# Output products of a recurrence in two runs, short operands padded to the whole array, and modulation products of two loads together

## The chip, the cores and the metric

The kernel runs on one core of one Trainium2 chip. The metric is the device time of one execution in microseconds (us). A core has a matrix engine (TensorE, "PE" in the profile), a vector engine (VectorE, "DVE"), a scalar engine (ScalarE, "ACT"), a general engine (GpSimd, "POOL") and SyncE ("SP"), which here only issues transfers between main memory and the on-chip buffer. The engines run side by side, each works through its own list of instructions in order, and they wait for each other on semaphores. TensorE multiplies a stationary operand, loaded first (weight load, "PEld"), with a moving one and writes into accumulator banks (PSUM).

## The reference

One layer of a decoder step for 256 prompt tokens and 8 samples of 8 tokens: 320 token columns in all, with D = 2048 channels and 16 heads of 64. In short:

```
mod = silu(c) @ w_ada + b_ada                     # six vectors: shift, scale, gate for mixer and FFN
h   = rms_norm(x) * (1 + scale_m) + shift_m
z   = h @ w_in                                    # columns of all branches, 9472 wide
r, k, v, decay, a, g = ...                        # token-shifted columns, two low-rank factors of width 64
kk  = k * k_k / norm over the head                # removal keys
per token: S = S*diag(w) - (S kk)(a*kk)^T + v k^T ;  o = S r          # state per head, 64 x 64
y_a = (group_norm(o) + bonus) * g @ w_branch_a
y_b = (gelu(u) * (W_s @ layer_norm(gelu(v)) + b)) @ w_branch_b
x   = x + gate_m * ((sig0*y_a + sig1*y_b) @ w_out)
x   = x + gate_f * FFN(rms_norm(x) ...)           # SwiGLU, width 5632
y   = rms_norm(x)
```

It returns the outputs, the states after the step, the token-shift rows and the normalised v rows of the samples.

## The kernel before

Channels lie on the 128 partitions and tokens on the free axis. A float32 product with a weight matrix is made of three passes over exact high and low parts (L155 to L157): `wsplit` (L133) makes the high part of a loaded weight tile on ScalarE (wh) and the low part on VectorE (wl). A weight tile is up to 1 MB, there are three buffers for tiles (wst) and four for each of the parts. These *main products* have 128 x 128 stationary tiles and 320 moving columns.

The program has these stages. First the modulation of the mixer, the transposed input (L378) and the projection to the recurrence's columns. Then quantities per token (`prep1` to `prep3`, L685 to L805): decay and rate from low-rank factors (L691, L692), sums over a head for the norms of the removal keys (L721) and their return to all rows (L735). Then the recurrence, in chunks of 64 tokens: chunk 4 holds all samples, chunks 0 to 3 the prompt. For a chunk, `chunk_load` fetches what `prep3` wrote to main memory; `chunk_g` makes causal products of keys and queries, two heads' halves at a time on either half of the partitions (L896, L897); `chunk_w` turns keys and values to have tokens on partitions (L910, L915, L916); `chunk_t` completes a triangular inverse (L933, L938); `chunk_x` applies the state and the inverse (L950, L956); `chunk_o` makes the outputs, the state's part and the chunk's own part for each of 8 pairs of heads and each half (L977, L978); `chunk_s` advances the state (L966); `chunk_n` is the group norm (L166). Last come branch b, branch a, the output projection and the FFN.

Between these steps `fill(n)` (L1074) puts quarter units of main products into the program, so that TensorE has work while a chain of small steps runs on other engines, and in proportion it takes from the list `adas` the loads of the other four modulation vectors: `ada_group` (L344) and `ada_cols` (L305), 16 loads of 1 MB for each vector; behind each load stand four products, one for each quarter of the array's columns (L318). Some of these loads are taken out one by one around the norm ahead of the FFN (L1313, L1324) and in its first units (L1412).

The order in each engine's list isn't that of the text: a planner sets it when the program is built, by executing it on its own model of costs and taking what is ready by priority. A block under `manual_schedule` keeps the written order among its own instructions on the named engines; where other instructions fall between stays the planner's. Transfers issued by `ld` stand in SyncE's list, those by `sd` in GpSimd's; each list is worked through in order, so an issue that waits for its buffer holds back all behind it. A tile of a pool (`tag`, `bufs`) takes one of `bufs` buffers and waits until an earlier owner is done.

Of the kernel before, what the change touches and what calls it, by code (L numbers as in the profile page):

```python
# [13 lines left out]
F32 = mybir.dt.float32  # L14
# [35 lines left out]
# columns of the two packed parameter tiles  # L50
# [5 lines left out]
def body(ctx, tc, I, O):  # L56
    """Channels lie on partitions and tokens on the free axis: columns 0..255 are the prompt, 256 + 8*s + t the
    samples.  A float32 product with a weight matrix runs as three float32r passes over exact high and low parts."""
# [27 lines left out]
    # ------------------------------------------------------------------ constants  # L86
# [34 lines left out]
    # ------------------------------------------------------------------ DRAM scratch  # L121
# [10 lines left out]
    # ------------------------------------------------------------------ weights: load, split in two exact parts  # L132
# [30 lines left out]
    def both(ps, w, parts):  # L163
        """ps = w^T (hi + lo), w being exact in float32r"""
# [35 lines left out]
    def tile_units(src, ktiles, xh, xl, group, evict, kx0):  # L200
        """the column tiles of one group, each over all k"""
# [14 lines left out]
    # ================================================================== mixer sub-layer  # L216
# [11 lines left out]
    # ---- conditioning and parameters  # L228
# [6 lines left out]
    ld(xt[0:64, 2], I["x_sample"].rearrange("s t d -> (s t) d"))  # L235
    pr1 = st.tile([128, 128], F32, name="pr1")
# [15 lines left out]
    def params2():  # L252
# [5 lines left out]
        # token-shift states ahead of every sample, zeros ahead of the prompt  # L258
# [8 lines left out]
    # ---- ada: the conditioning rows stationary, four column tiles of the array at once  # L267
# [4 lines left out]
    def ada_half(k0, nk):  # L272
        """shift_m and scale_m of the channel tiles k0..k0+nk-1, nk <= 2: each array tile takes a quarter of k"""
# [31 lines left out]
    def ada_cols(pool, kb, c0s, w, dsts):  # L305
        """array tile j takes w of the modulation columns"""
        box = {}

        def load(kq):
            if kq == 0:  # L310
                box["pa"] = ps_ax(512)
            wt = (pool or late["w"])().tile([128, kb, 4 * w], F32, tag="wa", name="wa", bufs=2)
# [3 lines left out]
            for kk in range(kb):  # L316
                for j in range(4):
                    PE.matmul(box["pa"][32 * j:32 * j + 32, 0:w], cT[:, kq * kb + kk], wt[:, kk, j * w:j * w + w], start=kq + kk == 0, stop=kq * kb + kk == KT - 1,  # L318
                              tile_position=(0, 32 * j))
# [24 lines left out]
    def ada_group(g):  # L344
        """one of the other modulation vectors"""
# [22 lines left out]
    def h_raw(k0, nk):  # L368
        """normalised, channels on partitions"""
# [4 lines left out]
        def turned(k):  # L374
            px = [ps_ax(NP), ps_ax(T - NP)] if k == 0 else [ps_ax(T)] * 2
            for c, n in enumerate(rows):
                o = px[c // 2][:, c % 2 * 128:c % 2 * 128 + n] if k == 0 else px[0][:, c * 128:c * 128 + n]
                PE.transpose(o, xt[0:n, c, k * 128:k * 128 + 128], ident[0:n, 0:n])  # L378
# [22 lines left out]
    # ---- RWKV columns: the sum over k runs in segments, as the modulation arrives  # L401
# [28 lines left out]
    # the groups of four columns in turn, each time over the channel tiles that have come since its last turn  # L430
# [54 lines left out]
    # ------------------------------------------------------------------ main products beside the recurrence  # L485
    mp_g, mpool = open_pool("mp", "left")

    # gMLP constants
    def ws_prep():
# [10 lines left out]
        for s in range(NS):  # L500
            V.tensor_scalar(gp["wsS"][:, :, s], pr[0:64], bm8[0:64, s:s + 1], None, op0=MUL)
# [3 lines left out]
    # bm8[p, s] = 1 where (p mod 64) // 8 == s ; rep8[a, (s, t)] = 1 where a == t  # L505
# [6 lines left out]
    def v_evict(i, ps):  # L512
# [4 lines left out]
        for c, n in enumerate(rows):  # L517
            PE.transpose(pt[0:n, c], gv[:, c * 128:c * 128 + n], ident)
        act(gp["vtm"][:, 0:2, i * 128:i * 128 + 128], pt[:, 0:2], AF.Copy)
        act(gp["vtm"][0:64, 2, i * 128:i * 128 + 128], pt[0:64, 2], AF.Copy)  # L520
# [30 lines left out]
    def gm_open():  # L551
# [3 lines left out]
        gp["wsS"] = gm.tile([64, 8, NS, TS], F32, name="wsS")  # L555
# [907 lines left out]
```

## Time and profile before

| | |
|---|---|
| median of 3 runs | 2081.64 us (2080.64 to 2081.8) |
| profiled execution, first to last instruction (span) | 2079.3 us; its time with start and end isn't listed apart |
| TensorE busy | 2031.0 us, 98%, 14578 products |
| VectorE, ScalarE, GpSimd busy | 51%, 38%, 7% |
| mean granted TensorE clock | 0.984 |
| transfers | 421 MB, 202 GB/s in the mean |

Busy is the time in which at least one instruction of an engine is under way; products overlap, so the distance between starts tells more than a length. "128*64 128x64" is 128 rows and 64 columns of the array, and a moving operand of 128 partitions with 64 columns. An fp32 product stands as two records. Lines named L155 are lines of the kernel; a helper's line (L79, L82) stands for all that it records. In tables of stretches the columns are: stretch, its length, busy time (instructions), granted clock, share of time that the transfer engines were busy, GB/s.

### The profile page before, as it was taken

The numbers are of one execution on the slowest core, as the hardware profiler recorded it, in microseconds if no ns is written. First come the engines' busy times: TensorE is split into PE (matmuls) and PEld (weight loads), VectorE is DVE, ScalarE is ACT, GpSimd is POOL, SyncE is SP. The second block draws the span as 40 slices with busy tenths as digits, with TensorE's granted clock in tenths as the row PEclk, the third lists the DMA queues.
The fourth block names the chain that finished last, engine by engine and source line by source line (L and its number), as shares of the span: only waits on it lengthen the run. The fifth ranks groups of instructions, "written<-read, shape, count | busy, mean of one in ns | idle before, by whom it ended". The sixth has DMA issues, their size and how long they took to land.

```text
span 2079.3 us, 35907 instructions
## 1 busy us (share of the span) xinstructions
PE 2031.0 (98%) x14578; PEld 1860.3 (89%) x14578; DVE 1058.4 (51%) x1904; ACT 794.2 (38%) x1168; POOL 136.6 (7%) x243
## 2 busy tenths in 40 slices
PE   6999999999999999999999999999999999999997
PEld 4788988889787888888888889999999999999997
DVE  2565668759453453445347334445345345445345
ACT  6323376534233233434326233233333332332344
POOL 1000002230330001100000000000000000000000
PEclk9999999999998999999999999999999999999998
DMA  9888447597587757888875775454544454453552
GB/s 273 288 290 299 144 149 256 196 230 214 163 242 196 214 203 242 326 315 292 309 260 180 245 234 173 123 169 128 157 153 145 152 172 126 149 173 123 156 168 71
DMA packets 303109, 420.99 MB, mean 202 GB/s; under 512 B 62310, under 2 KB 202584, under 8 KB 294112
## 3 DMA queue, kind: packets, MB, share of 16 engines
q1 hardware_dynamic: 293856, 388.20, 57.7%
q0 software_dynamic: 9088, 30.50, 4.5%
q8 instruction: 115, 1.88, 0.4%
q14 instruction: 50, 0.41, 0.1%
HBM read 390.40 MB, written 28.23 MB: 201 GB/s over the span
## 4 chain that ended last, share of the span: by engine, by line
PE 86%; issue 4%; DVE 3%; DMA 3%; POOL 1%; SPq 1%; ACT 1%; DVEq 0%; POOLq 0%; ACTq 0%
PE mm L155 25%; PE mm L157 24%; PE mm L156 24%; PE ax L318 4%; PE ax L977 1%; PE ax L978 1%; PE ax L286 1%; DVE wl L79 1%; DMA d_mb<-gt 1%; DMA gt<-d_sg 1%; DMA xt<-in_x_prompt 0%; DVE tm L79 0%; DMA Lr<-d_l 0%; POOL we L1049 0%; PE ax L378 0%
## 5 line engine op out<-in xcount | busy, mean ns | idle before, releaser
L79 DVE TENSOR_TENSOR wl<-ws,wh 128x1024 fp32r<-128x1024 f32 (+1 forms) x304 | 362.7, 1214 | 320.3 <-ACT wh L82 317.6
L82 ACT ACTIVATE wh<-ws 128x1024 fp32r<-128x1024 f32 (+1 forms) x304 | 306.2, 1041 | 462.5 <-PE mm L156 338.3
L155 PE MATMUL mm<-h2h,wh 128*128 128x320 f32 x1408 | 435.9, 310 | 0.7 <-ACT h2h L82 0.7
L156 PE MATMUL mm<-h2l,wh 128*128 128x320 f32 x1408 | 435.1, 309 | 0.1
L157 PE MATMUL mm<-h2h,wl 128*128 128x320 f32 x1408 | 435.1, 309 | 0.0
L79 DVE TENSOR_TENSOR wl<-wf,wh 128x1024 fp32r<-128x1024 f32 x176 | 215.1, 1224 | 327.7 <-ACT wh L82 323.1
L155 PE MATMUL mm<-hh,wh 128*128 128x320 f32 x1184 | 377.0, 320 | 1.2 <-ACT wh L82 0.6
L157 PE MATMUL mm<-hh,wl 128*128 128x320 f32 x1184 | 368.4, 313 | 1.5 <-DVE wl L79 1.4
L156 PE MATMUL mm<-hl,wh 128*128 128x320 f32 x1184 | 369.4, 312 | 0.0
L82 ACT ACTIVATE wh<-wf 128x1024 fp32r<-128x1024 f32 x176 | 185.2, 1058 | 381.9 <-PE mm L156 352.9
L155 PEld LDWEIGHTS mm<-h2h,wh 128*128 128x128 f32 x1408 | 264.1, 188 | 11.7 <-issue 7.5
L156 PEld LDWEIGHTS mm<-h2l,wh 128*128 128x128 f32 x1408 | 264.3, 188 | 0.4 <-DVE h2l L79 0.4
L157 PEld LDWEIGHTS mm<-h2h,wl 128*128 128x128 f32 x1408 | 264.3, 188 | 0.0
L155 PEld LDWEIGHTS mm<-hh,wh 128*128 128x128 f32 x1184 | 224.0, 190 | 31.4 <-issue 22.6
L157 PEld LDWEIGHTS mm<-hh,wl 128*128 128x128 f32 x1184 | 223.9, 190 | 9.8 <-issue 6.3
L156 PEld LDWEIGHTS mm<-hl,wh 128*128 128x128 f32 x1184 | 224.8, 190 | 5.3 <-issue 4.4
L155 PE MATMUL mm<-fh,wh 128*128 128x320 f32 x704 | 217.0, 308 | 0.0
L157 PE MATMUL mm<-fh,wl 128*128 128x320 f32 x704 | 216.8, 308 | 0.0
L156 PE MATMUL mm<-fl,wh 128*128 128x320 f32 x704 | 216.8, 308 | 0.0
L155 PEld LDWEIGHTS mm<-fh,wh 128*128 128x128 f32 x704 | 131.9, 187 | 0.0
L156 PEld LDWEIGHTS mm<-fl,wh 128*128 128x128 f32 x704 | 131.9, 187 | 0.0
L157 PEld LDWEIGHTS mm<-fh,wl 128*128 128x128 f32 x704 | 131.9, 187 | 0.0
(357 smaller groups left out, 2342.7 us busy)
## 6 DMA issues: line engine op xcount, KB each, us to landing
wf<-in_w_ffn_in SPq DMA_DIRECT2D x352, 256.0 KB, 3.0
ws<-in_w_in SPq DMA_DIRECT2D x64, 1024.0 KB, 7.2
wa<-in_w_ada SPq DMA_DIRECT2D x64, 1024.0 KB, 6.3
ws<-in_w_ffn_out SPq DMA_DIRECT2D x40, 1024.0 KB, 5.1
wa<-in_w_ada SPq DMA_DIRECT2D x48, 512.0 KB, 4.9
ws<-in_w_out SPq DMA_DIRECT2D x16, 1024.0 KB, 5.4
d_w<-pk POOLq DMA_DIRECT2D x8, 1120.0 KB, 5.4
wa<-in_w_ada SPq DMA_DIRECT2D x32, 256.0 KB, 4.7
```

The lines of the kernel that those rows point to most:

```text
L79: return (eng or V).tensor_tensor(out, a, b, op=op)
L82: return A.activation(out, in_, fn, **kw)
L155: PE.matmul(ps, hi[:, k, sl], xh[:, kx + a + k], start=f, stop=False)
L156: PE.matmul(ps, hi[:, k, sl], xl[:, kx + a + k], start=False, stop=False)
L157: PE.matmul(ps, lo[:, k, sl], xh[:, kx + a + k], start=False, stop=e)
L286: PE.matmul(box["pa"][32 * j:32 * j + 32, 0:w], cT[:, 4 * q + j], wt[:, j], start=q == 0, stop=q == 3, tile_position=(0, 32 * j))
L318: PE.matmul(box["pa"][32 * j:32 * j + 32, 0:w], cT[:, kq * kb + kk], wt[:, kk, j * w:j * w + w], start=kq + kk == 0, stop=kq * kb + kk == ...
L977: PE.matmul(po[lo:lo + 64, j], SV[:, j, h], b["M"][:, j, h, 64:128], start=True, stop=False)
L978: PE.matmul(po[lo:lo + 64, j], b["VS"][lo:lo + 64, j, h], b["D"][lo:lo + 64, j], start=False, stop=True)
```

## The change

It consists of several edits.

1. In `chunk_o` the output products stand in two runs (all of the state's part, then all of the chunk's own part) into one accumulator bank, in the written order.
2. In `chunk_g` the causal products keep the written order, which alternates the two halves.
3. Operands with fewer than 128 rows or columns are padded with zeros, or with other columns whose results aren't read: the low parts of the low-rank factors, the selection matrices for the head sums and their return, the third token tile of the transposed input and of the transposes in the v branch and at the end, and the gMLP's product for the samples.
4. In `chunk_w` the values of two head pairs are turned by one 128 x 128 transpose; for this `chunk_load` brings them in four transfers in place of one, into one buffer.
5. In `ada_cols` the products of the late modulation wait for two loads and then run together; the loads have three buffers in place of two.
6. Some tiles share buffers (tp, sl, xg, so2), and comments and descriptions go.

The core of the diff (removed comments and the renamed slices that follow from it are left out):

```diff
     def chunk_o(c, SV):
         po = ps_ax(NJ, 64)
-        for j in range(NJ):
-            for h, lo in ((0, 0), (1, 64)):
-                PE.matmul(po[lo:lo + 64, j], SV[:, j, h], b["M"][:, j, h, 64:128], start=True, stop=False)
-                PE.matmul(po[lo:lo + 64, j], b["VS"][lo:lo + 64, j, h], b["D"][lo:lo + 64, j], start=False, stop=True)
+        with tc.manual_schedule(engines={mybir.EngineType.PE}):
+            for j in range(NJ):
+                for h, lo in ((0, 0), (1, 64)):
+                    PE.matmul(po[lo:lo + 64, j], SV[:, j, h], b["M"][:, j, h, 64:128], start=j == 0, stop=False, skip_group_check=True)
+            for j in range(NJ):
+                for h, lo in ((0, 0), (1, 64)):
+                    PE.matmul(po[lo:lo + 64, j], b["VS"][lo:lo + 64, j, h], b["D"][lo:lo + 64, j], start=False, stop=j == NJ - 1, skip_group_check=True)
...
     def chunk_g(c):
-            for jj in range(4):
-                j = 4 * q + jj
+            with tc.manual_schedule(engines={mybir.EngineType.PE}):
+                for jj in range(4):
+                    j = 4 * q + jj
...
     def chunk_load(c):
-        b["v"] = cp.tile([128, NJ, 64], F32, name="vc", tag="vc", bufs=nb)
-        ld(b["v"], d_w[:, c, :, 4])
+        b["v"] = cp.tile([128, NJ // 2, 2, 64], F32, name="vc", tag="vc", bufs=1)
+        for a in range(2):
+            for h in range(2):
+                ld(b["v"][64 * a:64 * a + 64, :, 1 - h], d_w[64 * h:64 * h + 64, c, a::2, 4])
...
     def chunk_w(c):
-        for j in range(NJ):
-            PE.matmul(pv[64:128, j], b["v"][0:64, j], ident[0:64, 0:64], start=True, stop=True)
-            PE.matmul(pv[0:64, j], b["v"][64:128, j], ident[64:128, 64:128], start=True, stop=True)
+        for i in range(NJ // 2):
+            PE.transpose(pv[:, 2 * i:2 * i + 2].rearrange("p j v -> p (j v)"), b["v"][:, i].rearrange("p h t -> p (h t)"), ident)
...
-    def ada_cols(pool, kb, c0s, w, dsts):
-        box = {}
+    def ada_cols(pool, kb, c0s, w, dsts, kr=1, bufs=2):
+        box, held = {}, []
         def load(kq):
-            if kq == 0:
-                box["pa"] = ps_ax(512)
             (the tile, now with bufs=bufs, and its load)
-            for kk in range(kb):
-                for j in range(4):
-                    PE.matmul(box["pa"][32 * j:32 * j + 32, 0:w], cT[:, kq * kb + kk], wt[:, kk, j * w:j * w + w], ...)
+            held.append((kq, wt))
+            if len(held) < kr:
+                return
+            if "pa" not in box:
+                box["pa"] = ps_ax(512)
+            for q, wt in reversed(held):
+                for kk in range(kb):
+                    for j in range(4):
+                        k = q * kb + kk
+                        PE.matmul(box["pa"][32 * j:32 * j + 32, 0:w], cT[:, k], wt[:, kk, j * w:j * w + w], ...)
+            held.clear()
...
     def ada_group(g):
-        return ada_cols(None, 1, [g * D], 512, dsts)
+        return ada_cols(None, 1, [g * D], 512, dsts, kr=2, bufs=3)
...
     def prep1(j):
             PE.matmul(p, ups["h"][:, i, js], lact[i], start=True, stop=False)
-            PE.matmul(p, ups["l"][lo, js], lact[i][lo], start=False, stop=True)
+            PE.matmul(p, ups["l"][:, i, js], lact[i], start=False, stop=True)
...
-        PE.matmul(kn["p"][0:32], hsel[:, j], sq, start=j % 4 == 0, stop=j % 4 == 3)
+        PE.matmul(kn["p"], hsel[:, 2 * NJ - 2 - 2 * j:2 * NJ - 2 - 2 * j + 128], sq, start=j % 4 == 0, stop=j % 4 == 3)
...
-        rs = rp.tile([64, F], F32R, name="rs", tag="rn", bufs=2)
+        rs = rp.tile([128, F], F32R, name="rs", tag="rn", bufs=2)
+        G.memset(rs[64:128].bitcast(F32), 0.0)
...
-            for c, n in enumerate(rows):
-                PE.transpose(o, xt[0:n, c, k * 128:k * 128 + 128], ident[0:n, 0:n])
+            for c in range(3):
+                PE.transpose(o, xt[:, c, k * 128:k * 128 + 128], ident)
...
-        PE.matmul(pm[:, NP:T], gp["vtm"][0:64, 2, sl], gp["wsS"][:, g].rearrange("p s t -> p (s t)"), start=True, stop=True)
+        PE.matmul(pm[:, NP:T], gp["vtm"][:, 2, sl], gp["wsS"][:, g].rearrange("p s t -> p (s t)"), start=True, stop=True)
...
     def turn():                     # v_evict in the same way
-            for c, n in enumerate(rows):
-                PE.transpose(pt[0:n, c], xg[:, c * 128:c * 128 + n], ident)
+            for c, t0 in enumerate((0, 128, T - 128)):
+                PE.transpose(pt[:, c], xg[:, t0:t0 + 128], ident)
-            V.tensor_copy(yy["b"][:, i * 128:i * 128 + 128], pt[0:64, 2])
+            V.tensor_copy(yy["b"][:, i * 128:i * 128 + 128], pt[64:128, 2])
...
-        tp = p2.tile([128, NS, TS], F32, name="tp", tag="tp", bufs=2)
+        tp = p2.tile([128, NS, TS], F32, name="tp", tag="tp", bufs=1)
-                            sl = p2.tile([128, T], F32, name="sl", tag="sl", bufs=2)
+                            sl = p2.tile([128, T], F32, name="sl", tag="hf2", bufs=2)
-                xg = p2.tile([128, T], F32, name="xg", tag="xg", bufs=2)
+                xg = p2.tile([128, T], F32, name="xg", tag="hf2", bufs=2)
-        so = cp.tile([128, NJ, 64], F32, name="so2", tag="so2", bufs=2)
+        so = cp.tile([128, NJ, 64], F32, name="so2", tag="Lc", bufs=1)
```

Memsets on GpSimd write the zeros of the padded parts (of the input tile, of the low factors, of the selection matrices, of the gMLP's v tile and of its sample matrix).

More of the change, by code (lines that the diff above doesn't have):

```diff
@@ L303, in ada_half @@
         return [lambda q=q: load(q) for q in range(4)] + [flush]
-    def ada_cols(pool, kb, c0s, w, dsts):
-        box = {}
+    def ada_cols(pool, kb, c0s, w, dsts, kr=1, bufs=2):
+        box, held = {}, []
         def load(kq):
-            if kq == 0:
-                box["pa"] = ps_ax(512)
-            wt = (pool or late["w"])().tile([128, kb, 4 * w], F32, tag="wa", name="wa", bufs=2)
+            wt = (pool or late["w"])().tile([128, kb, 4 * w], F32, tag="wa", name="wa", bufs=bufs)
             cw = 4 * w // len(c0s)
@@ L315, in load @@
                 ld(wt[:, :, ci * cw:ci * cw + cw], w_ada[kq * kb * 128:(kq + 1) * kb * 128, c0:c0 + cw].rearrange("(k p) n -> p k n", p=128))
-            for kk in range(kb):
-                for j in range(4):
-                    PE.matmul(box["pa"][32 * j:32 * j + 32, 0:w], cT[:, kq * kb + kk], wt[:, kk, j * w:j * w + w], start=kq + kk == 0, stop=kq * kb + kk == KT - 1,
-                              tile_position=(0, 32 * j))
+            held.append((kq, wt))
[7 more added lines that the diff above has]
+                        k = q * kb + kk
+                        PE.matmul(box["pa"][32 * j:32 * j + 32, 0:w], cT[:, k], wt[:, kk, j * w:j * w + w], start=kq == kr - 1 and q == kq and kk == 0,
+                                  stop=kq * kb + kb == KT and q == held[0][0] and kk == kb - 1, tile_position=(0, 32 * j))
+            held.clear()
         def flush():
@@ L516, in v_evict @@
         pt = ps_ax(3, 128)
[L517 to L518 removed]
+        for c, t0 in enumerate((0, 128, T - 128)):
+            PE.transpose(pt[:, c], gv[:, t0:t0 + 128], ident)
         act(gp["vtm"][:, 0:2, i * 128:i * 128 + 128], pt[:, 0:2], AF.Copy)
[L520 removed]
+        act(gp["vtm"][0:64, 2, i * 128:i * 128 + 128], pt[64:128, 2], AF.Copy)
     def v_norm():
@@ L554, in gm_open @@
         gp["wsT"] = gm.tile([128, 8, 128], F32, name="wsT")
-        gp["wsS"] = gm.tile([64, 8, NS, TS], F32, name="wsS")
+        gp["wsS"] = gm.tile([128, 8, NS, TS], F32, name="wsS")
         gp["vtm"] = gm.tile([128, 3, 1024], F32, name="vtm")
+        G.memset(gp["wsS"][64:128], 0.0)
+        G.memset(gp["vtm"][64:128, 2], 0.0)
         gp["wsr"] = gm.tile([128, 8, 128], F32, name="wsr", tag="gA")
@@ L625, in ups_load @@
         ups["h"] = rp.tile([128, 2, 512], F32R, name="uph", tag="uph")
-        ups["l"] = rp.tile([128, 512], F32R, name="upl", tag="upl")
+        ups["l"] = rp.tile([128, 2, 512], F32R, name="upl", tag="upl")
         act(ups["h"], w, AF.Copy)
         for i, lo in enumerate((0, 64)):
-            tt(ups["l"][lo:lo + 64], w[lo:lo + 64, i], ups["h"][lo:lo + 64, i].bitcast(F32), SUB)
+            G.memset(ups["l"][64 - lo:128 - lo, i].bitcast(F32), 0.0)
+            tt(ups["l"][lo:lo + 64, i], w[lo:lo + 64, i], ups["h"][lo:lo + 64, i].bitcast(F32), SUB)
     mG = mpool.tile([128, 2, 2, 64], F32, name="mG")
@@ L698, in prep1 @@
         sg4[j] = lg
-    hsel = rp.tile([128, NJ, 32], F32, name="hsel")
+    hsel = rp.tile([128, 2 * NJ - 2 + 128], F32, name="hsel")
+    G.memset(hsel, 0.0)
     for h, lo in ((0, 0), (1, 64)):
-        G.affine_select(out=hsel[lo:lo + 64], in_=ones[lo:lo + 64, 0:32].unsqueeze(1).to_broadcast([64, NJ, 32]), compare_op=ALU.is_equal, fill=0.0, base=-h, pattern=[[-2, NJ], [1, 32]],
-                        channel_multiplier=0)
+        G.memset(hsel[lo:lo + 64, 2 * NJ - 2 + h:2 * NJ - 1 + h], 1.0)
     bself = rp.tile([64, NJ, 2, 64], F32, name="bself", tag="pk", bufs=2)
-    bsel = rp.tile([64, NJ, 2, 64], F32R, name="bsel")
+    bsel = rp.tile([128, NJ, 2, 64], F32R, name="bsel")
+    G.memset(bsel[64:128].bitcast(F32), 0.0)
     for lo in (0, 32):
@@ L710, in body @@
                             channel_multiplier=1)
[L711 removed]
+    G.tensor_copy(bsel[0:64], bself)
     kn = {}
@@ L1391, in turn @@
             pt = ps_ax(3, 128)
-            for c, n in enumerate(rows):
-                PE.transpose(pt[0:n, c], xg[:, c * 128:c * 128 + n], ident)
+            for c, t0 in enumerate((0, 128, T - 128)):
+                PE.transpose(pt[:, c], xg[:, t0:t0 + 128], ident)
             act(yy["a"][:, :, i * 128:i * 128 + 128], pt[:, 0:2], AF.Copy)
-            V.tensor_copy(yy["b"][:, i * 128:i * 128 + 128], pt[0:64, 2])
+            V.tensor_copy(yy["b"][:, i * 128:i * 128 + 128], pt[64:128, 2])
     pend = []
```

16 lines of the change are left out of this document (7 added, 9 removed).

## The prediction

> **What bounds the kernel now.** I read the page's first parts, then the chain of waits, then TensorE's timeline around the edited lines, and last the transfers.
>
> ```profile
> span 2079.3 us, 35907 instructions
> PE 2031.0 (98%) x14578; PEld 1860.3 (89%) x14578; DVE 1058.4 (51%) x1904; ACT 794.2 (38%) x1168; POOL 136.6 (7%) x243
> PEclk9999999999998999999999999999999999999998
> PE 86%; issue 4%; DVE 3%; DMA 3%; POOL 1%; SPq 1%; ACT 1%; DVEq 0%; POOLq 0%; ACTq 0%
> ```
>
> TensorE is busy for 98% of the span and makes 86% of the chain that ends last; VectorE and ScalarE are far from it. A busy figure says nothing of how well the time is used, so I go by the distance between starts. A microsecond taken out of TensorE's list is worth a microsecond wherever TensorE doesn't then wait for something else.
>
> The five calls of the output product (L977, L978) take these stretches, from the first product to the start of the next other one. The columns are length, TensorE busy with its products, granted clock, transfers' share and rate.
>
> ```profile
> 543.55:553.08 9.53, 9.53 (x65) 0.81 0.41 154
> 648.07:661.64 13.57, 13.57 (x110) 0.64 0.21 74
> 700.88:710.56 9.68, 9.68 (x65) 0.79 0.24 96
> 748.13:757.51 9.38, 9.38 (x65) 0.83 0.01 3
> 784.80:795.66 10.86, 10.86 (x65) 0.67 0.60 231
> ```
>
> That is 53.0 us for 5 x 64 small products (an fp32 product shows as two records; the second stretch also holds some 40 others). Transfers nearly stop in three of them, since the weight buffers are full: TensorE alone is late. The timeline shows why:
>
> ```profile
> 700.88 0.33 PE L977 MATMUL ax<-M,SVp 128*64 128x64 f32 x2
> 701.13 0.33 PE L978 MATMUL ax<-Dt,VS 64*64 64x64 f32 x2
> ```
>
> Each pair takes 0.25 us, and the shape changes from 128x64 to 64x64 each time. Products of the same shapes that stand in a run of 32 are quoted next: 1.15 us to the last one's end.
>
> ```profile
> 722.20 1.15 PE L950 MATMUL ax<-SVp,M 128*64 128x64 f32 x32
> 774.86 1.15 PE L956 MATMUL ax<-xx,Tc 64*64 64x64 f32 x32
> ```
>
> **The change part by part.**
>
> *Output product in two runs.* 32 records of L950's shape, then 32 of L956's: 2 x 1.15 = 2.3 us a chunk, 11.5 for five. The others in the second stretch stay; at full clock I put them at 1.6. So 53.0 - 13.1 = 39.9 us gained. The far end: records that do not overlap at all cost about 0.13 us each (1.05 for eight, quoted below at L896), 8.4 a chunk, a gain of 9. I take the near end, since shape, alternation of the two halves and the one accumulator bank are those of L950 and L956.
>
> *The clock.* Each of the five stretches begins at full clock and loses it after some 4 to 6 us (the 0.64 to 0.83 above). What follows each until the clock is back, added up, and two stretches just before one drop:
>
> ```profile
> sum 16.45, PE 16.45; mean PE 3.29
> 645.10:648.07 2.97, 2.97 (x75) 1.00 0.15 56
> 648.07:651.90 3.83, 3.83 (x36) 1.00 0.02 4
> ```
>
> In these 16.45 us the clock stood at 0.50, so up to 8.2 is lost there; I take 7. The 75 small products in 2.97 us did not cost the clock; the drop came at the end of the second stretch, with 36 in 3.83, at 651.9. The run after the change is of the dense kind and lasts 2.3 us, so I expect no drop. Ends: 0 and 8.2.
>
> *Late modulation, two loads together.* One visit, and the one place where two visits already stand together:
>
> ```profile
> 718.55 0.31 PE L157 MATMUL mm<-hh,wl 128*128 128x320 f32 x1
> 718.79 1.06 PE L318 MATMUL ax<-wa,cT 128*32 128x512 f32 x8
> 719.78 0.42 PE L155 MATMUL mm<-hh,wh 128*128 128x320 f32 x1
> 720.04 0.31 PE L156 MATMUL mm<-hl,wh 128*128 128x320 f32 x1
> ```
>
> ```profile
> 1239.78 1.92 PE L318 MATMUL ax<-wa,cT 128*32 128x512 f32 x16
> 1241.63 0.42 PE L155 MATMUL mm<-h2h,wh 128*128 128x320 f32 x1
> ```
>
> A main product is followed by the next after 0.15 us, but after 0.24 where the shape changes, and the first one behind a visit holds 0.26. So a visit costs 0.09 + 0.99 + 0.11 = 1.19 us, two 2.38; the double one 0.09 + 1.85 + 0.10 = 2.04. 0.34 a pair; four groups of 16 loads are 32 pairs, one already double: 31 x 0.34 = 10.5. The far end, where other work splits the pairs, is 0.
>
> *Operands padded to 128.* The decay and rate products (L691, L692), eight times:
>
> ```profile
> 277.90 0.31 PE L691 MATMUL ax<-lact,uph 128*128 128x328 f32 x1
> 278.14 0.41 PE L692 MATMUL ax<-lact,upl 64*128 64x328 f32 x1
> 278.48 0.42 PE L691 MATMUL ax<-lact,uph 128*128 128x328 f32 x1
> 278.83 0.41 PE L692 MATMUL ax<-lact,upl 64*128 64x328 f32 x1
> 279.18 0.41 PE L155 MATMUL mm<-hh,wh 128*128 128x320 f32 x1
> ```
>
> 1.28 us for four products that in one shape need about 4 x 0.15, and 0.10 on the first main product: 0.78 x 8 = 6.3. The removal key's return product (L735), eight times, is one such 64-row visit: 0.09 + 0.34 + 0.10 against 0.15, so 3.0. Its sums (L721), eight: two changes of shape, about 0.2 each time; 2 with some lost on slower full-width records. The input transposes (16 tiles) and the sample product of the gMLP (8) give up one visit each, 24 x 0.2 = 5. The transposes in the last norm and the v branch already write a full-height tile for two of three thirds; I put them at 0. Together 16.3; the far end is half, if padding slows the records as it may for L721.
>
> *Value transposes.* 80 + 80 products of 64 rows become 20 whole transposes.
>
> ```profile
> L915 PE MATMUL ax<-ident,vc 64*64 64x64 f32 x80 | 5.7, 221 | 0.0
> 624.50 0.61 PE L910 MATMUL ax<-ident,KB 128*128 128x128 f32 x4
> ```
>
> L915 and L916 run beside each other: 5.7 us for both, plus 0.2 a chunk for the changes of shape: 6.7. Four whole transposes 0.54 to 0.61: 5 x 0.54 = 2.7. Gain 4. The Trainium skill speaks against such padding: TensorEngine Tiling (Array Packing), section Key Properties, says that tiles work independently and in parallel, which a whole-array product gives up. The trace bears the rule out inside a run (the 0.11 us for two records below), and by it alone nothing would be gained and the sum would be 4 smaller; here four instructions replace 32, and that decides.
>
> *Causal products in emission order (L896, L897).*
>
> ```profile
> 731.24 0.27 PE L897 MATMUL ax<-M,KB 64*128 64x128 f32 x1
> 731.35 0.27 PE L896 MATMUL ax<-M,KB 64*128 64x128 f32 x1
> ...
> 732.02 1.05 PE L896 MATMUL ax<-M,KB 64*128 64x128 f32 x8
> 733.49 1.13 PE L897 MATMUL ax<-M,KB 64*128 64x128 f32 x8
> ```
>
> Alternating, two records start every 0.11 us; alone, 16 took 2.1. Paired these 16 take 0.9: 1.2 a chunk, 6 for five. Order also binds the first half's products to the later loads of the second; the planner can put main products between, as now. Far end 0.
>
> *What is added.* Three more value loads a chunk, with what queues behind them on SyncE:
>
> ```profile
> 606.52 0.93 SPq L870 DMA_DIRECT2D vc<-d_w  x1
> 600.00:950.00 350.00, 342.28 (x2882) 0.94 0.78 255
> 850.00:900.00 50.00, 49.44 (x337) 1.00 0.89 319
> 0.00:220.00 220.00, 201.66 (x1487) 1.00 0.83 279
> ```
>
> At 0.6 to 0.9 us an issue that is about 2 us of SyncE's queue a chunk, behind which wait the triangular block, the modulation and the weights. It is free where that queue waits anyway; I book 1. The single value buffer is freed by the transposes long before its next load, and the memsets on GpSimd (7% busy) stand early: 0. The shared buffers (tp, sl, xg, so2) change owners between phases: 0. With the modulation in pairs, only a load and no product stands ahead of the FFN norm's sums: one visit less of cover, 1 us. Last, the transfers: 600 to 950 us moves 255 GB/s at a share of 0.78, 273 us of transfers. The terms above shorten that stretch by about 51 (output product 31.5, clock 6, causal 4.8, values 3.2, modulation 5.4), to 299, a share of 0.91. The busiest row ran at 0.89 with TensorE waiting a little; 273 / 0.89 = 307, so I book 8. Ends: 0, and all 51.
>
> **Sum.** 39.9 + 7 + 10.5 + 16.3 + 4 + 6 = 83.7, less 10: 73.7. Span 2079.3 - 73.7 = 2005.6. The execution profiled lies 2.3 us under the runs' median of 2081.64, which I add back: 2008.
>
> **The rivals.**
>
> *Transfers take over (24%).* At the 279 GB/s of the first 220 us, the 89.3 MB of 600 to 950 need 320 us: 21 lost instead of 8, 2021; the limit, no gain there at all, is 2051. For it: the shares above. Against: 319 GB/s with TensorE at 49.44 of 50, and the idle transfers inside the five stretches.
>
> *The clock drops all the same (9%).* Without the 7, and with the five runs at half clock (11.5 more): 2027. The Trainium skill, TensorE: Matmul & The Clock Gate, Part 4, says that transposes do not count as busy, and more of the work is transposes now. The 75 records quoted at clock 1.00 speak against it.
>
> *The planner breaks the runs (6%).* By hand only the order is fixed, not what falls between. With half of the output gain, the causal gain and the pairs gone (20 + 6 + 10.5): 2045. In the second stretch other products already stand inside.
>
> *Slower: pairs hold SyncE's queue (4%).* A modulation load waits for its buffer, and weights wait behind it:
>
> ```profile
> SPq L315 <- PE ax L318: 88.7, 11, 23.9
> wa<-in_w_ada SPq DMA_DIRECT2D x64, 1024.0 KB, 6.3
> ```
>
> That queue already stood 88.7 us in 11 such waits between 600 and 800. If every pair made TensorE wait half a landing (3.2 us), 32 of them cost 101: 2109. It decides from 73.7 / 32 = 2.3 us a pair. Against it: with three buffers a load waits for a pair at least two turns back, no closer than now, and today's waits hardly reach TensorE (2% idle).
>
> **How the numbers follow.** The forecast has 57%, its own range 1998 to 2018. Outside 1996 to 2036 I leave the planner, the slow rival and part of the transfers' tail. Faster holds all but the last rival and a scrap: 0.95; within 0.2% 0.01 (about what a measurement of this kernel can tell from no change); slower 0.04.
>
> **What would show it.** Right: each output product about 2.3 us with one change of shape inside; clock 1.00 from 600 to 800; 32 visits of 16 modulation records at 1.85; no 64-row records on L692's and L735's successors. Wrong: output runs well over 3 us, TensorE waits on weights (wh, wl) in 600 to 950 adding up to over 10 us, or a granted clock of 0.5 right behind the runs.

## The result, and the profile after

| | us, median | lowest to highest | ratio to before, 95% interval |
|---|---|---|---|
| before | 2081.72 | 2080.64 to 2085.22 | |
| after | 2025.81 | 2025.0 to 2027.71 | 0.9727, 0.9713 to 0.974 |
| forecast | 2008 | 1996 to 2036 | 0.965 |

The change is worth 55.9 us, 18 less than forecast. First the head of the changed kernel's profile page.

```profile
span 2023.4 us, 35669 instructions
PE 1964.0 (97%) x14438; PEld 1830.8 (90%) x14438; DVE 1060.0 (52%) x1904; ACT 794.7 (39%) x1168; POOL 141.3 (7%) x254
PEclk9999999999998999999999999999999999999998
```

TensorE is busy for 67.0 us less (2031.0 before), but the span is only 55.9 shorter: outside its busy time there are now 59.4 us, where there were 48.3. That is the first sign of work saved and not cashed.

The output product stands as forecast. Chunk 1 in the timeline (start, length, line, operands, count):

```profile
673.89 1.15 PE L993 MATMUL ax<-M,SVp 128*64 128x64 f32 x32
674.97 1.15 PE L996 MATMUL ax<-Dt,VS 64*64 64x64 f32 x32
676.05 1.15 PE L980 MATMUL ax<-VS,Wt 128*64 128x64 f32 x32
```

Two runs take 2.16 us from start to start (9.68 before in this chunk), with one change of shape between them. So do the padded decay products and a pair of modulation loads:

```profile
270.25 0.31 PE L701 MATMUL ax<-lact,uph 128*128 128x328 f32 x1
270.40 0.32 PE L702 MATMUL ax<-lact,upl 128*128 128x328 f32 x1
...
270.85 0.31 PE L155 MATMUL mm<-hh,wh 128*128 128x320 f32 x1
...
691.66 1.92 PE L325 MATMUL ax<-wa,cT 128*32 128x512 f32 x16
693.51 0.42 PE L155 MATMUL mm<-hh,wh 128*128 128x320 f32 x1
```

0.60 us for the four products and 1.85 for the pair, both as worked out beforehand.

To see where the gain lies I cut the span at main products, those of L155 to L157, which come in one order in every kernel here: "2500 to 3500" is the time from the start of the 2500th to that of the 3500th. In brackets the part of it at half clock, without the last 10 us or so at the end of the span, where TensorE has nothing left to do. (Start times and clock windows are from the trace.)

```
main products     before         after         gain
0 to 1300         271.8          267.3          4.5
1300 to 2000      139.2          127.9         11.3
2000 to 2500      102.3 ( 6.8)   104.1 ( 6.8)  -1.8
2500 to 3500      306.9 (44.4)   265.3 (13.7)  41.6
3500 to 4600      199.0 ( 3.4)   198.2 ( 3.4)   0.8
4600 to 5800      211.0          210.5 ( 6.8)   0.5
5800 to the end   849.0          849.9         -0.9
```

The gain sits in two places: the decay products (1300 to 2000) and the chunks with the output product (2500 to 3500). The late modulation, which runs from 2900 to 5900 or so and was to bring 10.5, shows nothing. And one place in the chunks looks new:

```profile
630.32 1.03 PE L996 MATMUL ax<-Dt,VS 64*64 64x64 f32 x28
631.28 1.93 PE L325 MATMUL ax<-wa,cT 128*32 128x512 f32 x16
633.13 0.33 PE L996 MATMUL ax<-Dt,VS 64*64 64x64 f32 x2
...
634.87 0.50 PE L166 MATMUL ax<-ocl,cmat 128*128 128x512 f32 x1
636.72 0.51 PE L166 MATMUL ax<-sqh,bmean 128*128 128x512 f32 x1 [1.35 <-ACT sqh L82]
...
641.29 1.97 PE L970 MATMUL ax<-xx,Tc 64*64 64x64 f32 x32 [0.78 <-DVE xx L966]
643.20 0.63 PE L155 MATMUL mm<-hh,wh 128*128 128x320 f32 x1
```

Around chunk 0's output product (whose second run the planner did break, with little harm) there is no main product from 621.86 to 643.20, so the group norm's wait for ScalarE (1.35) is open. The stretches around it, around a second wait at 661 and behind a third at 1049 (columns: length, busy time of TensorE, its weight loads, VectorE, ScalarE, GpSimd, granted clock, transfers' share, GB/s):

```profile
634.50:637.30 2.80, 1.45 (x7) 0.67 (x5) 2.71 (x5) 1.84 (x3) 0.00 (x0) 1.00 0.97 363
637.30:647.50 10.20, 9.30 (x85) 6.65 (x88) 7.84 (x8) 3.83 (x5) 0.00 (x0) 0.50 1.19 265
658.20:661.20 3.00, 0.81 (x6) 0.42 (x4) 0.42 (x1) 2.75 (x5) 0.00 (x0) 1.00 1.15 374
661.20:664.60 3.40, 3.18 (x11) 2.95 (x12) 2.36 (x2) 1.11 (x2) 0.00 (x0) 0.50 0.99 378
1050.40:1053.80 3.40, 3.40 (x19) 0.68 (x17) 2.07 (x6) 2.30 (x4) 0.00 (x0) 0.51 0.20 36
```

Each time TensorE has been waiting, it goes to half clock for 3.4 or 10.2 us. In this execution the wait of 1.35 us costs 1.35 + 5.1; the last section shows another execution, where the same wait costs no clock.

My first theory for the missing 18 us was SyncE's queue: modulation loads that wait for their buffer hold the weights behind them. The rival was the transfers' rate, which is high here, in bursts:

```profile
574.00:604.00 30.00, 29.98 (x221) 28.97 (x220) 19.35 (x29) 11.51 (x15) 7.20 (x12) 1.00 1.03 325
604.00:634.00 30.00, 27.43 (x425) 21.82 (x426) 10.48 (x21) 10.31 (x19) 0.54 (x1) 1.00 0.78 217
634.00:664.00 30.00, 25.33 (x205) 19.47 (x200) 19.48 (x24) 9.97 (x14) 0.86 (x1) 0.78 1.09 319
```

A third was that the terms themselves were smaller than I put them.

### The profile page after: what moved, and what is told of

Same layout as the page of the kernel before. It is cut to its first block, busy times and chain, and to the rows that moved or that the text cites. A ratio compares the mean times of both kernels' runs of the same rounds, so it can differ in the third digit from the quotient of the medians.

```text
span 2023.4 us, 35669 instructions
## 1 busy us (share of the span) xinstructions
PE 1964.0 (97%) x14438; PEld 1830.8 (90%) x14438; DVE 1060.0 (52%) x1904; ACT 794.7 (39%) x1168; POOL 141.3 (7%) x254
## 4 chain that ended last, share of the span: by engine, by line
PE 61%; DMA 1%; DVE 1%; ACT 1%; issue 1%; SPq 0%; DVEq 0%; ACTq 0%
PE mm L155 19%; PE mm L157 19%; PE mm L156 19%; PE ax L325 2%; DMA gt<-d_sg 1%; DMA um<-d_um 0%; ACT wh L82 0%; DVE wl L79 0%; DMA d_mb<-gt 0%; PE ax L1411 0%; PE ax L1280 0%; DVE gt L79 0%; PE ax L1311 0%; PE ax L980 0%; PE ax L993 0%
## 5 line engine op out<-in xcount | busy, mean ns | idle before, releaser
L155 PE MATMUL mm<-h2h,wh 128*128 128x320 f32 x1408 | 436.3, 310 | 2.1 <-ACT h2h L82 2.1
L157 PE MATMUL mm<-h2h,wl 128*128 128x320 f32 x1408 | 435.3, 309 | 0.0
L155 PE MATMUL mm<-hh,wh 128*128 128x320 f32 x1184 | 376.4, 320 | 2.9 <-ACT wh L82 2.2
L157 PE MATMUL mm<-hh,wl 128*128 128x320 f32 x1184 | 368.3, 313 | 1.3 <-DVE wl L79 1.1
L155 PEld LDWEIGHTS mm<-h2h,wh 128*128 128x128 f32 x1408 | 264.8, 188 | 8.1 <-issue 2.5
L157 PEld LDWEIGHTS mm<-h2h,wl 128*128 128x128 f32 x1408 | 264.7, 188 | 0.0
L155 PEld LDWEIGHTS mm<-hh,wh 128*128 128x128 f32 x1184 | 224.3, 190 | 23.7 <-issue 12.4
L157 PEld LDWEIGHTS mm<-hh,wl 128*128 128x128 f32 x1184 | 223.7, 189 | 7.6 <-issue 3.5
L155 PE MATMUL mm<-fh,wh 128*128 128x320 f32 x704 | 217.0, 308 | 0.0
L157 PE MATMUL mm<-fh,wl 128*128 128x320 f32 x704 | 216.9, 308 | 0.0
L157 PEld LDWEIGHTS mm<-fh,wl 128*128 128x128 f32 x704 | 131.9, 187 | 0.1
L155 PEld LDWEIGHTS mm<-fh,wh 128*128 128x128 f32 x704 | 131.9, 187 | 0.0
```

The costliest lines, as they stand in the source:

```text
L155: PE.matmul(ps, hi[:, k, sl], xh[:, kx + a + k], start=f, stop=False)
L157: PE.matmul(ps, lo[:, k, sl], xh[:, kx + a + k], start=False, stop=e)
```

## The experiments

Twelve kernels in three groups, each group on one chip beside the kernel before. All stand against before by their ratio; differences of some 4 us between two profiles are not told apart, since two executions of the changed kernel differ by as much in one stretch and by 8 in the span (last experiment).

### The output runs alone, and all but the output runs

```
o_alone = before, with the new chunk_o:
 -  for j, h:  matmul(po, SV, M, stop=False); matmul(po, VS, D, stop=True)
 +  with tc.manual_schedule(engines={PE}):          (around both runs)
 +  for j, h:  matmul(po, SV, M, start=j == 0, stop=False)
 +  for j, h:  matmul(po, VS, D, start=False, stop=j == NJ - 1)
o_back  = after, with the old chunk_o
```

> The kernel before, with one part of the change only: the output product in two runs. By the prediction's own terms it gains 39.9 (the products) and 7 (the clock), less about 4 for the transfers that then have less time: 2081.7 - 43 = 2039. Theory of SyncE's queue: the long output product of chunk 0 had covered a stretch in which no weights of the main products arrive (in the profile of the kernel before, the weight tile of visit 130 was ready at 676.3, 54 us behind the one before it), and what it covered, some 11 us, is given back: 2050. If the two runs were worth less in themselves, the five stretches would show more than 2.5 us each.

> The changed kernel with the output product alternating as before, all else as changed. If the two runs bring all that the prediction put down, 39.9 and 7, it is slower by 47: 2073. If the rest of the change had already filled the queue and the transfers, so that part of the gain of the runs was given back in waits, it is slower by about 35: 2061, and TensorE's waits on weights between 600 and 800 are smaller than in the changed kernel.

Measured: 2032.67 us for the runs alone (2028.75 to 2033.63; ratio 0.9764, 0.975 to 0.9777), a gain of 48.4; 2074.29 without them (2070.34 to 2079.16; 0.9969, 0.9958 to 0.9981), 48.5 slower than the changed kernel (49 and 50 by the ratios). The same price from both sides, and it is what the forecast had for the products and the clock, 46.9: from the 2500th to the 3500th main product the stretch went from 306.91 to 260.11, by 46.8. First the kernel before in that stretch, then the kernel with the runs alone, its page's head and the same stretch.

```profile
513.33:820.24 306.91, 302.50 (x2618) 246.08 (x2617) 143.95 (x186) 90.18 (x130) 51.63 (x67) 0.93 0.69 208
```

```profile
span 2030.2 us, 35910 instructions
PE 1983.9 (98%) x14578; PEld 1828.1 (90%) x14578; DVE 1059.4 (52%) x1904; ACT 794.9 (39%) x1168; POOL 134.1 (7%) x243
...
511.77:771.88 260.11, 255.45 (x2619) 213.89 (x2617) 144.50 (x186) 90.19 (x130) 51.09 (x67) 1.00 0.82 246
```

The clock is 1.00 in it. So nothing of this part is given back, the theory that the queue would take 11 us from it (2050) falls, and everything else in the change together is worth 7 us, where the forecast had 36.8 - 10 = 26.8. These two spans show how the rest was lost. From the runs alone to the whole change TensorE's busy time falls from 1983.9 to 1964.0, by 19.9. At half clock it spent 10.2 us in the one kernel (two windows) and 30.7 in the other (six windows, the last at the end of the span left out in both), so about 10.2 us of busy time were added by the clock, and the work itself shrank by some 30.1 of the 36.8. Time outside busy grew from 46.3 to 59.4, by 13.1. 30.1 - 10.2 - 13.1 = 6.8: the work was saved, waits and the clock drops behind them took three quarters of it.

### Part by part

```
mod_single = after, ada_group:  -  kr=2, bufs=3      +  kr=1, bufs=2
g_back     = after, chunk_g:    -  with tc.manual_schedule(engines={PE}):
v_back     = after, chunk_load: -  4 loads of b["v"] [128, NJ // 2, 2, 64]
                                +  ld(b["v"], d_w[:, c, :, 4])          (one buffer)
                    chunk_w:    -  4 transposes      +  16 products of 64 rows
mod_v_back = mod_single and v_back together, two value buffers
```

> The changed kernel with each load of the late modulation on its own visit and two buffers, as before. The prediction's term says slower by 10.5 and faster by 1 for the cover ahead of the FFN norm: 2035. If the pairs' gain is eaten where they stand (the count of main products shows about 1 us instead of 5.8 between the 3500th and the 4600th), slower by 3 to 5 only: 2030. If holding SyncE's queue is a loss, not slower at all: 2026 or less.

> The changed kernel with the order of the causal products left to the planner again. The prediction's term says slower by 6: 2032. By the stretches in the profile after (2.4 to 2.7 us a chunk) the order is worth 0.7 to 1.1 a chunk, 4 in all: 2030. Rival: binding the order to the later loads of the second half keeps main products out of the gap at chunk 0, and the free order is no slower: 2026 or less.

> The changed kernel with the value tiles loaded by one transfer a chunk and turned by 64-row products, as before (one buffer). By the prediction's terms (4 gained by the transposes, 1 lost to issue) slower by 3: 2029. If the four loads, which in the profile after take 3.2 to 3.8 us of SyncE's queue a chunk ahead of the weights, cost TensorE more than the transposes save, as the stretch from the 2900th to the 3100th main product suggests (5 us lost there against the kernel with the output runs alone), it is faster: 2022.

> The changed kernel with both the late modulation and the value tiles as before; what stays are the output runs, the padded operands and the order of the causal products. The prediction's terms: slower by 10.5 + 4 - 3 = 11: 2037. If both parts only feed waits on weights in a stretch that SyncE's queue and the transfers bound, it is no slower than the changed kernel, and by the gain that the padded products show (11 between the 1300th and the 1900th main product on top of the 48 of the output runs) it comes to 2032.7 - 11.3 = 2021.

| kernel | us | ratio, 95% interval |
|---|---|---|
| modulation singly | 2026.06 | 0.9738, 0.9725 to 0.9751 |
| causal order free | 2028.47 | 0.9745, 0.973 to 0.976 |
| value tiles as before | 2025.21 | 0.9714, 0.9691 to 0.9736 |
| both as before | 2023.39 | 0.9707, 0.9687 to 0.9728 |
| the change | 2025.81 | 0.9727, 0.9713 to 0.974 |

None can be told from the changed kernel. So the pairs and the value transposes, forecast at 10.5 and 4, are worth nothing together (2037 was forecast without them), and the order of the causal products (6) is not told from nothing. What is left beside the runs is the padding. Its worth repeats from run to run: from the 1300th to the 2000th main product every kernel with it takes 127.9 us, the two without it 139.2. That is 11.3, the sum of 6.3, 3.0 and 2.

That the pairs did what they were meant to do, and still brought nothing, is in the stretch behind the chunks, from the 3500th to the 4600th. First the changed kernel, then the one with single loads:

```profile
764.71:962.91 198.20, 190.93 (x1310) 170.71 (x1309) 92.99 (x142) 80.89 (x127) 14.55 (x27) 0.99 0.88 312
```

```profile
768.70:964.96 196.26, 193.16 (x1310) 169.41 (x1309) 93.53 (x142) 80.83 (x127) 14.55 (x27) 0.99 0.90 318
```

TensorE has 2.2 us less to do with pairs, but is idle for 7.3 instead of 3.1. That holds across the kernels: in this stretch those with single loads are idle for 3.1 to 5.5 us, those with pairs for 6.5 to 7.9 (two kernels that move work into or out of the stretch, `no_mod_c` and `spread` below, left out). Both run at 312 to 318 GB/s and a share of 0.9, as full as the busiest row of the prediction.

### Queue or rate: the modulation's loads on another queue, and out of the chunks

```
wa_pool  = after, in chunks 0 to 3:   -  nc.sync.dma_start(wt ...)   +  nc.gpsimd.dma_start(wt ...)
no_mod_c = after:   -  R1, R2, R3, R4 = 0.3, 0.2, 0.2, 0.36
                    +  R1, R2, R3, R4 = 0.0, 0.3, 0.3, 0.6
```

> The changed kernel with the late modulation's loads issued by GpSimd instead of SyncE during chunks 0 to 3 (the same transfers, another queue). If the gain of the pairs is lost because a modulation load that waits for its buffer holds the weights behind it in SyncE's queue (47 us of such waits between 575 and 770), the stretch without main products at 624 to 643 closes and the kernel is faster by 6 to 11: 2015 to 2020. If the transfers' rate is what takes the gain, nothing changes: 2026, with the same GB/s in the stretch.

> The changed kernel with no late modulation beside chunks 0 to 3: its loads and products move into the branches and the output projection. Eight pairs leave the stretch from the 2500th to the 3500th main product, 8 x 2.05 = 16.4 us of TensorE and 16.8 MB of transfers. If the transfers' rate makes the waits there, the stretch shrinks by more than the products: 265.3 - 16.4 - 11 = 238, with idle time of 4 or less and no half clock. If the chain of the chunks itself (VectorE, ScalarE, the chunk's own loads) makes them, the idle time stays at 12 and the stretch comes to 249 or more, since the modulation no longer fills it. The whole kernel: not faster, as the products stand elsewhere: 2015 to 2030.

On GpSimd's queue: 2031.93 (2028.39 to 2036.82; 0.9756, 0.9733 to 0.9778), no faster and in the trace worse: the stretch takes 269.2. TensorE's longest wait there, in the view of waits, and the time from issue to landing of the keys (KB) and weights in the transfers of 574 to 665:

```profile
PE ax L912 <- DMA KB<-d_w: 8.2, 1, 8.2
...
ws<-in_w_in SPq DMA_DIRECT2D x5, 1024.0 KB, 11.9
KB<-d_w SPq DMA_DIRECT2D x4, 256.0 KB, 12.5
```

In the changed kernel, same view, same stretch of time:

```profile
wa<-in_w_ada SPq DMA_DIRECT2D x9, 1024.0 KB, 7.7
ws<-in_w_in SPq DMA_DIRECT2D x5, 1024.0 KB, 10.6
KB<-d_w SPq DMA_DIRECT2D x3, 256.0 KB, 9.4
```

With no modulation in the chunks (one load left at the edge):

```profile
ws<-in_w_in SPq DMA_DIRECT2D x9, 1024.0 KB, 9.0
wa<-in_w_ada SPq DMA_DIRECT2D x1, 1024.0 KB, 16.3
KB<-d_w SPq DMA_DIRECT2D x4, 256.0 KB, 7.0
```

And the stretch from the 2500th to the 3500th main product, first of the changed kernel, then without the modulation:

```profile
499.37:764.71 265.34, 252.90 (x2479) 212.46 (x2477) 145.76 (x186) 90.71 (x130) 52.80 (x67) 0.97 0.80 245
```

```profile
500.84:737.48 236.64, 229.64 (x2346) 204.07 (x2345) 145.36 (x185) 90.38 (x129) 52.36 (x67) 1.00 0.71 203
```

The stretch shrinks by 28.7: 16.4 for the products of eight pairs, 6.9 since the 13.7 us at half clock are gone, 5.4 since the idle time falls from 12.4 to 7.0. The expectation of the rate's theory was 238 with 4 idle, that of the chunks' own chain 249 or more with 12. In the 91 us of the landing times nine modulation loads and five weight tiles came in with the modulation, one and nine without it.

But these numbers don't explain the hole at 622 to 643. The kernel with the runs alone, which has no such hole, got the same nine and five in 91 us:

```profile
wa<-in_w_ada SPq DMA_DIRECT2D x9, 1024.0 KB, 7.6
ws<-in_w_in SPq DMA_DIRECT2D x5, 1024.0 KB, 8.3
```

What the hole follows is the value tiles' four loads together with the modulation in SyncE's queue. In the kernels with the output runs the longest distance between two main products from the 2500th to the 3500th, and TensorE's idle time there, are in us:

```
                                              distance        idle
four value loads and modulation on SyncE      18.7 to 23.6    12.1 to 14.4    (changed kernel twice, modulation
                                                                               singly, causal order free, both NB1)
one value load, modulation singly or paired   9.7, 10.2       7.5, 6.7        (value tiles as before, both as before)
one value load, modulation singly, more main
  products beside the chunks (spread, below)  4.6             5.1
four value loads, modulation on GpSimd        9.8             17.2
four value loads, no modulation               5.5             7.0
runs alone                                    7.7             4.7
```

So going back to one value load wins some 5 us of idle time in this stretch, and the stretch takes 260.6 and 261.5 instead of 264.4 to 266.9, as the second theory in the expectation for the value tiles had it. The whole kernel's time does not show it: with the value tiles as before the other stretches are longer by as much. Nor is all of it the hole: TensorE waits for GpSimd's tile `we` at chunk 4 for 4.0 to 4.3 us in the kernels with four value loads and for 2.0 in those with one. Whether the four loads act by their time in SyncE's queue or by the order that the planner then chooses stays open.

Taking SyncE's queue away from the modulation wins nothing in all: the hole shrinks to 9.8 us, as the queue's theory had it, but the landings become longer and 8.2 us of waiting for keys come in its place. It is not a clean cut: with the modulation gone from that queue the planner issued four weight tiles ahead of the keys, and these held the queue in their turn. Nor does a full burst make waits by itself: the kernel with the runs alone has the same bursts (weight tiles land in 8.3 us, keys in 8.0) and 4.7 us of idle time in the stretch, with some 9 us more of TensorE's own work to lay over them. How much of the loss is rate and how much the order of the loads stays open.

The whole kernel without modulation in the chunks takes 2021.54 us (2020.63 to 2025.31; 0.9709, 0.9693 to 0.9726), against 2026.76 (2026.2 to 2033.31) for the changed kernel on the same chip: 5.2 faster, with no overlap of the runs. It is faster than the kernel before and the changed one.

### The cover ahead of the FFN norm

```
nb1_2, nb1_0 = after:  -  NB1 = 1     +  NB1 = 2   and   NB1 = 0
      while len(adas) > 15 + NB1:
          adas.popleft()()
```

> The changed kernel with one more modulation load ahead of the sums of the FFN norm, so that a pair of products stands before them as cover. If the lost cover is what the stretch from the 5000th to the 5400th main product shows (2.4 lost; waits of 1.40 at 1047.5 and 1.80 at 1054.8, and two windows of 3.4 us at half clock), faster by 2 to 4: 2022 to 2024. If the waits there are the norm's own chain, whatever stands ahead, 2026.

> The changed kernel with two modulation loads, and so a pair of products, ahead of the sums of the FFN norm. (The run with the other number had in fact put none there: the modulation was taken down to a remainder, and that remainder was raised.) If lost cover is what that place shows, TensorE's wait of 1.37 ahead of the sums goes, one of the two half-clock windows with it, and the kernel is faster by 2 to 4. If the norm's own chain decides, no change within 1 us.

The first run missed its aim: the number is what remains, so 2 takes away the load that stood there. 2029.96 (2026.09 to 2030.85; 0.9735, 0.9713 to 0.9756). With 0, a pair stands ahead of the sums: 2024.36 (2022.47 to 2026.87), 2.4 under the changed kernel on the same chip, though their runs overlap. The trace shows more: 1.6 are won from the 4600th to the 5800th main product, though one pair more stands there, and 2.0 behind it, where that pair is gone; 3.6 in all, and 3.9 against the second execution of the changed kernel (last experiment). First the changed kernel's timeline, then this one's:

```profile
1049.15 0.38 PE L1311 MATMUL ax<-ones,acc 128*128 128x1 f32 x2 [1.37 <-DVE acc L79]
...
1050.50 3.52 PE L325 MATMUL ax<-wa,cT 128*32 128x512 f32 x16
...
1057.09 1.38 PE L155 MATMUL mm<-h2h,wh 128*128 128x320 f32 x4 [2.06 <-ACT h2h L82]
```

```profile
1050.01 1.92 PE L325 MATMUL ax<-wa,cT 128*32 128x512 f32 x16
1051.86 0.38 PE L1311 MATMUL ax<-ones,acc 128*128 128x1 f32 x2
```

The wait of 1.37 is gone, and with it one of the two windows at half clock, in which the pair behind the sums took 3.52; the pair that now stands ahead of them takes 1.92.

### More main products beside the chunks, and the changed kernel again

```
spread = mod_v_back:   -  F_C = [4, 2, 2, 3, 2, 3, 2, 2]
                       +  F_C = [6, 2, 2, 3, 2, 5, 2, 2]
```

> The kernel with late modulation and value tiles as before (output runs, padded operands and the order of the causal products stay), with two more quarter units of main products at the start of chunk 0 and two more ahead of each output product, which else stand behind chunk 3. The same work and the same bytes, spread over more time. If the waits come from too much traffic for the time that is left beside the chunks, idle time from the 2500th main product on falls from 6.6 to under 4, and it is faster than the changed kernel by 5 to 8: 2018 to 2021. If the chain of the chunks makes them, no difference to the kernel without the spreading, about 2 us under the changed kernel.

> The changed kernel once more, unaltered, so that the next three stand beside it on one chip: ratio to the kernel before 0.973. From the 2500th to the 3500th main product, in the profile after: 265.3 us, with 12.4 us in which TensorE stood idle and 13.7 at half clock; the kernel with the output runs alone had 260.1, 4.5 and 0.

Spread: 2037.28 (2034.83 to 2040.89; 0.9783, 0.9765 to 0.9801), 10.5 slower than the changed kernel beside it. The idle time from the 2500th to the 3500th did fall, from 6.7 to 5.1 (with more main products in the chunks, less of chunk 3 lies in it). But the main products that stand behind chunk 3 were not spare: they cover the loads that follow (the modulation, and the input for the residual). With ten units fewer the timeline there shows

```profile
779.42 1.94 PE L325 MATMUL ax<-wa,cT 128*32 128x512 f32 x8 [3.14 <-DMA wa<-in_w_ada]
783.66 1.93 PE L325 MATMUL ax<-wa,cT 128*32 128x512 f32 x8 [2.30 <-DMA wa<-in_w_ada]
790.94 0.87 PE L1279 MATMUL ax<-ident,xt 128*128 128x128 f32 x3 [5.35 <-DMA xt<-in_x_prompt]
```

10.8 us of waits for transfers, and 17.1 us at half clock around them. Neither theory had this.

The changed kernel again: 0.9738 (0.9719 to 0.9757). Its profiled execution is the slowest of its four (2033.31). It has the same hole and the same waits, and 202.5 us instead of 198.2 from the 3500th to the 4600th, with 13.7 us at half clock instead of 3.4: that much differs between two executions.

## Why the prediction was right and wrong

The direction, the size's order and the largest terms were right; the time missed by 18 us, outside the likeliest case's own range (1998 to 2018) and inside the whole one.

- **Output product and clock tails, 39.9 + 7.** Right: 48.4 and 48.5 measured. The runs take 2.16 us and keep the clock, as the forecast said they would.
- **Padded operands, 16.3.** 11.3 of it shown (1300 to 2000); that the three terms add up to it to the tenth is luck, as each is rounded. For the x transposes and the gMLP's product 5 was put down; up to the 1300th main product TensorE's busy time is 2.2 shorter than with the runs alone, and from there on it isn't told apart.
- **Pairs, 10.5.** The term's working is right to the hundredth (2.05 instead of twice 1.19 in 26 undisturbed visits), its worth is nothing (mod_single). What failed is the step that counts TensorE time as time: from the 3500th to the 4600th main product the transfers run at 312 GB/s and the gain goes into idle time, and from the 4600th to the 5800th the lost cover at the FFN norm takes it (idle 3.4 us instead of 1.7, and 6.8 at half clock instead of none, against single loads).
- **Value transposes 4, causal order 6.** The four transposes take 0.53 us as forecast; neither part is told from nothing in time. From start to start, waits left out, the causal products take 12.5 us instead of 16.6, so they gain 0.8 a chunk; the forecast was 1.2.
- **The costs, 10.** This is the step that failed. "Transfers in 600 to 950: 8", with an end of 51: against the runs alone, 2500 to 4600 shows 9.8 us more idle time and 13.7 us more at half clock, 17 in all. The three added value loads a chunk, booked at 1, are a large part: some 5 us of idle time from the 2500th to the 3500th go when they do. The share of the transfers, on which the 8 rests, doesn't tell the kernels apart: the three slices above (1.03, 0.78, 1.09) stand at 1.09, 0.70 and 1.09 in the kernel with the runs alone, which lost little. "FFN cover: 1" came to 3.6 in the trace of the kernel that has it back. One step is missed in all of them: a wait was priced at its length, and the clock lost behind it was not priced at all. That is 10.2 us more in the profile after than with the runs alone, part of it chance (last section).
- **Chunk 4's keys.** Not in the sum: with the stretch ahead 11 us shorter the keys' load is late: TensorE waits 4.5 us for it (2.5 with the runs alone, 3.6 before), and 2000 to 2500 is 1.8 longer than before.
- **Rivals.** By its number "The clock drops all the same", 2027, is the nearest to 2025.8, and that is luck: the runs kept the clock, and the drops that came stand elsewhere, behind waits. "Transfers take over", 2021, fits from the 3500th to the 4600th main product, where the pairs' gain went into idle time at 312 GB/s; in the chunks rate and order of the loads are not told apart. The Trainium skill's rule quoted there (TensorE: Matmul & The Clock Gate, Part 4, transposes don't count as busy) isn't needed: the drops stand behind waits. "The planner breaks the runs" happened once, at chunk 0, for nothing much. "Pairs hold SyncE's queue" didn't make the kernel slower: the pairs come out at zero.

## What to carry to other kernels

Price a saving at the rate of what sets the pace where it stands: here 47 us of small products cashed in full, in stretches where the transfers were busy for 0.01 to 0.60 of the time, and the pairs' 10.5 us cashed for nothing, most clearly where the transfers were busy for 0.88. An edit that saves TensorE time and adds transfers to a queue has two terms: the four transposes are as short as forecast, and their loads took at least as much away. The whole time hid that; the stretch in which the edit stands showed it. And a wait that opens in the middle of dense work can cost its length and some microseconds of half clock, so cover at a joint (a norm, a stage's start) can be worth more than its wait says: at the FFN norm a pair of products ahead of a wait of 1.37 won 3.6 in the trace.

## What I had not expected of the hardware

Waits well below 3 us brought the half clock: 1.35 us at 636.72 was followed by 10.2 us at 0.50, 1.37 at 1049.15 by 3.4, 2.24 at 661.42 by 3.4. The Trainium skill (TensorE: Matmul & The Clock Gate, section Why this matters for your kernels) advises to keep idle gaps under some 3 us; that wasn't enough here, and the measurement decides. In the two stretches quoted first, TensorE was busy for 1.45 of 2.80 us and 0.81 of 3.00, so it is the busy part of the last microseconds rather than one gap that seems to count.

The kept traces bear this out in part. In each of them the half-clock windows begin whole multiples of 3.41 us apart. Cut into such steps, the twelve profiles that have the output runs show this of steps at full clock: of 36 in which TensorE was busy for less than 0.40 of the step, all were followed by half clock; of over 6700 with 0.70 or more, none; of the 96 between, 34. The wait of 1.35 us fell between. When the changed kernel ran again, the same wait with the same 1.45 us of work around it was followed by full clock:

```profile
639.23 0.50 PE L166 MATMUL ax<-sqh,bmean 128*128 128x512 f32 x1 [1.35 <-ACT sqh L82]
```

```profile
637.00:639.80 2.80, 1.45 (x7) 0.68 (x5) 2.71 (x5) 1.83 (x3) 0.00 (x0) 1.00 0.99 366
639.80:650.00 10.20, 7.80 (x99) 5.45 (x99) 9.01 (x9) 3.85 (x5) 0.00 (x0) 1.00 1.19 257
```

So the same wait cost clock in one execution and none in the other. Busy time isn't all that counts, either: in the two kernels with the alternating output product, ten steps that it filled completely were followed by half clock. Why is not shown.

An issue can itself take long. With the modulation on GpSimd's queue, one load of 256 KB took SyncE 8.93 us to issue and landed 17.0 us later, where the changed kernel's took 0.57 to issue. What held it isn't shown; the transfers were as full in the changed kernel (a share of 1.03 from 574 to 604, here 0.99):

```profile
589.79 8.93 SPq L879 DMA_DIRECT2D KB<-d_w  x1
...
KB<-d_w SPq DMA_DIRECT2D x1, 256.0 KB, 17.0
```
